# Attention and gated recurrence in one stage: products of pairs as reductions, backward states read from PSUM at the readout, and a written table of steps

## The chip, the cores and the metric

The kernel runs on one core of one Trainium2 chip. The metric is device time in microseconds (us) of one execution; the number compared is the median over several executions. Engines: PE is TensorE (matrix products and transposes), DVE is VectorE, ACT is ScalarE, POOL is GpSimd, and SP issues DMAs.

## The reference

One layer of a diffusion backbone on 2048 latent and 256 context tokens: a modulated norm, one input projection, two groups of heads, an output projection, then a SwiGLU network. The first group is softmax attention of 2048 queries over 2304 keys, 8 query heads on 2 key heads of width 64. The second is a gated linear recurrence with 4 heads of 128 by 128 states, run forward and backward:

```python
def gla_chunked(q, k, v, logf, s0):
    """S_t = diag(f_t) S_{t-1} + k_t v_t^T, o_t = S_t^T q_t, chunkwise."""
...
S, o = lax.scan(step, s0, (to_chunks(q), to_chunks(k), to_chunks(v), to_chunks(logf)))
...
ox_f, _ = gla_chunked(*hgrn2_prep(qx, ix, ffx, lb_l[0]), sc_f)
ox_b, _ = gla_chunked(*map(flip, hgrn2_prep(qx, ix, fbx, lb_l[1])), sc_b)
o = rmsnorm(o_f + flip(o_b), gain).reshape(Bn, T, HG_WIDTH)
return (o * jax.nn.silu(g.astype(jnp.float32))).astype(g.dtype)
```

Each latent scan starts from the last context state of its own direction. All is float32.

## The kernel before

The program has stages for the projections, then one stage that does the attention and the recurrence together, then the output projection and the SwiGLU network. The change lies in the middle stage.

**Attention.** The work is 64 items, two heads for 128 queries each; round r of the loop handles item r, so there are 64 rounds (r = 0 to 63), and a last pass that finishes. Names carry the item: `neg11_0_1_0` is item (query block 11, key head 0, second pair), its first head. A round has six places j = 0 to 5, one for each third of the 2304 keys of each of the two heads. At a place PE multiplies the scores s (128 x 768, two PSUM buffers), DVE takes their minimum `neg`, ACT takes the exponential into `pr` and sums it. After three thirds, ACT makes two factors `fac` for a head, POOL multiplies two thirds of `pr` by them, and the sums `ls` are multiplied by them later, in `finish`. PE transposes the `pr` of the item before into `pt` (two PSUM buffers, shared with `pof`), ACT or DVE copies them to `pf`, and at the round's end PE makes the products `av`, which ACT copies to `ot`; in the next round `finish` transposes `ot` into `pof`, and DVE divides (`oo`).

**Recurrence.** A `Unit` is one head and 512 latent tokens (u = 1 to 4) or the 256 context tokens (u = 0). `F03` is the forget gate of head 0, unit 3, with both directions as its last axis. A unit starts in the rounds 1, 4, 8, 11, 15 and so on to 53, and goes through seven levels, one a round. A level multiplies neighbouring pairs of decays into a tile T of half the size (DVE, line 685; at level 0 it reads F), and POOL and ACT make the next M, C and Q from T. F has one buffer, loaded by SP. The score blocks `pa` of two units at a time go into PSUM, and DVE copies them into A under a mask. After seven levels the unit is closed: `keys` transposes M and C (`pk`, copied to `kt` by ACT), `forward` multiplies with the values V (`psf`) and carries the state S along on DVE, `backward` makes the products `psb`, which ACT copies to `dS`. When a head's four units are closed, `head_out` carries the backward states `Sb` from the last chunk to the first on DVE, PE makes the outputs `po`, and each is normalised: ACT squares it, DVE sums, `rstd_from` makes the factor (on DVE the line `ms`, on POOL the power `rs`), DVE multiplies by QSCALE and then the output by `rs`, POOL multiplies by the gate `gt`, and SP stores it.

**What sets the order.** PE runs in the order of the code. For DVE, ACT, POOL and SP a scheduler sets the order from its own costs when the program is built; each engine then works through its queue in that order and waits where an operand is late. The pool `ps_h` has two PSUM buffers for all of pk, psf, psb, po, pa, pd and av. Closing and readout steps stand in a list, and `slots` spreads them over the places of a round by their number.

Of the kernel before, what the change touches and what calls it, by code (L numbers as in the profile page):

```python
# [16 lines left out]
P = 128  # L17
# [51 lines left out]
def block_kernel(ctx: ExitStack, tc: tile.TileContext, a: dict, out: bass.AP, dbg=None):  # L69
# [46 lines left out]
    def rstd_from(sp, ss, n, width, name):  # L116

        ms = sp.tile([P, width], F32, tag="ms", name=f"ms_{name}")
        nc.vector.tensor_scalar(ms, ss, 1.0 / n, EPS, op0=ALU.mult, op1=ALU.add)  # L119
        rs = sp.tile([P, width], F32, tag="rs", name=f"rs_{name}")  # L120
        nc.gpsimd.tensor_tensor(rs, ms, mhalf[:, :width], op=ALU.pow)  # L121
        return rs
# [446 lines left out]
    with ExitStack() as st:  # L569
# [17 lines left out]
        for lv in range(7):  # L587
            mf = up.tile([P, P], F32, tag="kt", name=f"mf{lv}", bufs=4)
            nc.sync.dma_start(mf, a["k_mask"][:, lv, :])
            nc.vector.tensor_copy(mask[:, lv, :], mf)  # L590
        class Unit:
# [59 lines left out]
            def level(self, pa=None):  # L651
# [32 lines left out]
                T3 = Tt[:, :nb, :].rearrange("p (j s) d -> p j s d", s=2)  # L684
                nc.vector.tensor_tensor(T2, T3[:, :, 0, :], T3[:, :, 1, :], op=ALU.mult)
# [3 lines left out]
            def keys(self, d):  # L689
# [6 lines left out]
                kt = up.tile([P, 512], F32, tag="kt", name=f"kt{h}{u}{d}", bufs=4)  # L696
# [17 lines left out]
            def backward(self, V):  # L714
# [8 lines left out]
        def head_out(h, V, S, units):  # L723
            Tt, dSb = units[0].T, units[0].dS
            coef, add = [Tt[:, 0, 1:2], dSb[:, 1, :]], dSb[:, 0, :]

            def chain(u):

                nonlocal coef, add
                out = []  # L730
                for c in range(3, -1, -1):
                    g = (u - 1) * 4 + c
                    Sb = smh.tile([P, P], F32, tag="Sb", name=f"Sb{h}_{g}", bufs=8)
                    nc.vector.scalar_tensor_tensor(Sb, coef[1], coef[0], add, op0=ALU.mult, op1=ALU.add)
                    coef, add = [units[u].T[:, c, 1:2], Sb], units[u].dS[:, c, :]
                    out.append(Sb)
                return out

            states = chain(4)
            for u in range(4, 0, -1):  # L740
                A, Q = units[u].A, units[u].Q
                po = ps_h.tile([P, 512], F32, tag="h", name=f"po{h}{u}")
                for c in range(3, -1, -1):
                    g = (u - 1) * 4 + c
                    cs = slice(c * P, (c + 1) * P)
                    nc.tensor.matmul(po[:, cs], A[:, cs], V[:, g + 2, :], start=True, stop=False)
                    nc.tensor.matmul(po[:, cs], Q[:, 1, cs], S[:, g + 2, :], start=False, stop=False)
                    nc.tensor.matmul(po[:, cs], Q[:, 0, cs], states[3 - c], start=False, stop=True)
                if u > 1:
                    states = chain(u - 1)  # L750
                o = up.tile([P, 512], F32, tag="o", name=f"o{h}{u}", bufs=2)
                o3 = o.rearrange("p (c v) -> p c v", v=P)
                p3 = po.rearrange("p (c v) -> p c v", v=P)
                nc.scalar.activation(o, po, AF.Square)
                ss = smh.tile([P, 4], F32, tag="ss4", name=f"sso{h}{u}")
                nc.vector.tensor_reduce(ss, o3, axis=AX.X, op=ALU.add)
                rs = rstd_from(smh, ss, P / QSCALE ** 2, 4, f"o{h}{u}")
                nc.vector.tensor_scalar(rs, rs, QSCALE, None, op0=ALU.mult)
                gt = up.tile([P, 4, P], F32, tag="gt", name=f"gt{h}{u}", bufs=1)
                nc.sync.dma_start(gt, s_g[h // 2][(u - 1) * 512:u * 512, (h % 2) * P:(h % 2 + 1) * P]  # L760
                                  .rearrange("(c p) v -> p c v", p=P))
                yield "open"
                nc.vector.tensor_tensor(o3, p3, rs[:, :, None].to_broadcast([P, 4, P]), op=ALU.mult)
                nc.gpsimd.tensor_tensor(o3, o3, gt, op=ALU.mult)
                nc.sync.dma_start(s_hg[h][(u - 1) * 512:u * 512].rearrange("(c p) v -> p c v", p=P), o3)
                yield

        class Recurrence:
# [3 lines left out]
            def __init__(self):  # L772
                self.lanes = {}
                self.steps, self.open = [], None
                self.V, self.S, self.units = {}, {}, {}
                self.starts = {1 + 7 * (n // 2) + 3 * (n % 2): n for n in range(4 * NH)}
                self.made = {}
                self.ctx = {}
# [16 lines left out]
            def closing(self, n, ctx):  # L795


                u, h = self.made.pop(n), n // 4
                V, S = self.V[h], None
                u.keys(0)  # L800
                yield
                u.keys(1)
                yield
                if n % 4 == 0:
                    S = self.S[h] = hp.tile([P, NTOK // P + 1, P], F32, tag="S", name=f"S{h}")
                    ctx.forward(V, S)
                    yield
                u.forward(V, self.S[h])
                yield
                u.backward(V)  # L810
                self.units[h][u.u] = u
                yield

            def closing_context(self, c):
                c.keys(0)
                yield
                c.keys(1)
                yield
                c.backward(self.V[c.h])
                self.units[c.h] = {0: c}  # L820
                yield

            def begin(self, r):
# [13 lines left out]
                n = self.starts.get(r - 7)  # L837
                if n is not None:
                    self.steps.append((self.closing(n, self.ctx.get(n // 4)), 4 + (n % 4 == 0)))
                n = self.starts.get(r - 3)  # L840
                if n is not None and n % 4 == 0:
                    self.steps.append((self.closing_context(self.ctx[n // 4]), 3))
                n = self.starts.get(r - 7)
                if n is not None and n % 4 == 3:
                    self.steps.append((head_out(n // 4, self.V[n // 4], self.S[n // 4], self.units[n // 4]), 4))

            def prepare(self, r):
                if r in self.starts:
                    self.made[self.starts[r]].prepare()

            def diagonal(self, r):
                if r in self.starts:
                    self.made[self.starts[r]].diagonal()
                    return True

            beside = iter(())

            def slots(self, r):


                due = sum(n for _, n in self.steps)
                left = next((i for i in range(1, 8) if r + i in self.starts), 2)
                k = -(-due // left)
                if r in self.starts:
                    return (0, 1, 4, 2)[:max(k, 2)]
                return ((), (2,), (1, 3), (0, 2, 4), (0, 1, 3, 4), (0, 1, 2, 3, 4))[min(k, 5)]

# [714 lines left out]
```

## Time and profile before

| | |
|---|---|
| Median of 3 runs | 3433.66 us (3432.63 to 3435.47) |
| The profiled execution | 3434.58 us, span 3432.8 us |
| PE busy in the span | 3246.4 us (95%) |
| DVE, ACT, POOL busy | 1940.3, 1605.0, 1781.2 us |
| Attention stage | 724 to 1885 us, PE busy 1049.6 |
| Mean granted PE clock | 0.982 |

The profile is one execution; lines such as L685 are those of the program before. A row of a group gives its busy time, the mean length of one in ns, and the time its engine stood idle just before such instructions, with what ended the waits. In a list of waits, the numbers are the total in us, how often, and the longest. PEclk is the clock that PE was granted, as a share of full speed; busy times of one engine include its time at a lower clock.

### The profile page before, as it was taken

What the parts mean: (1) busy time and instruction counts of PE and PEld (TensorE: products, weight loads), DVE (VectorE), ACT (ScalarE), POOL (GpSimd) and SP (SyncE); (2) the same over time, 40 slices, a digit from 0 to 9 for tenths busy, and PEclk for the clock granted to TensorE, in tenths of its full rate; (3) what the DMA queues carried; (4) which work ended last, traced back from release to release, by engine and by line L of the source; (5) the groups of instructions that cost most, each with busy time, mean ns of one, the idle gap of its engine ahead of it and who ended that gap; (6) DMA issues with size and microseconds to landing.
All of it is one profiled execution on the core that took longest, in us unless ns stands there. A gap on an engine that the chain in (4) does not pass through costs nothing. (4 is left out here: it accounts for less than half of the span.)

```text
span 3432.8 us, 54945 instructions
## 1 busy us (share of the span) xinstructions
PE 3246.4 (95%) x20220; PEld 2692.7 (78%) x20220; DVE 1940.3 (57%) x3302; ACT 1605.0 (47%) x3343; POOL 1781.2 (52%) x1616
## 2 busy tenths in 40 slices
PE   8999999989898888998999998999989989999998
PEld 5998987977777777777777887788867768888887
DVE  6444555136667667767666556444466753333566
ACT  4322322247676676776775214333344543333444
POOL 4322232137777777877755107767732257666322
PEclk9999999999999999999999999999989999999999
DMA  7244655421112102111104443544475543333764
GB/s 237 92 142 138 174 165 160 139 87 33 35 30 63 42 29 75 51 34 46 33 24 133 144 136 107 172 153 144 159 255 184 178 145 104 104 96 98 250 199 163
DMA packets 358623, 408.05 MB, mean 119 GB/s; under 512 B 31856, under 2 KB 249936, under 8 KB 358096
## 3 DMA queue, kind: packets, MB, share of 16 engines
q1 hardware_dynamic: 358352, 404.53, 37.0%
q8 instruction: 159, 2.61, 0.3%
q14 instruction: 112, 0.92, 0.1%
HBM read 274.92 MB, written 129.52 MB: 118 GB/s over the span
## 5 line engine op out<-in xcount | busy, mean ns | idle before, releaser
L933 DVE TENSOR_REDUCE neg<-s 128x1 f32<-128x768 f32 x384 | 365.8, 954 | 208.6 <-PE s L930 207.2
L945 POOL TENSOR_TENSOR pr<-pr,fac 128x768 f32<-128x768 f32 x256 | 372.8, 1478 | 127.8 <-ACT fac L941 124.0
L930 PE MATMUL s<-K,qs 128*128 128x512 f32 (+1 forms) x1536 | 374.7, 367 | 43.9 <-ACT pr L938 42.7
L938 ACT ACTIVATE pr<-s,neg 128x768 f32<-128x768 f32 x384 | 349.7, 911 | 95.3 <-DVE neg L933 69.0
L953 PE MATMUL pt<-identr,pr 128*128 128x128 f32 x2304 | 337.3, 279 | 46.2 <-DVE oo L989 21.6
L930 PEld LDWEIGHTS s<-K,qs 128*128 128x128 f32 x1536 | 265.4, 193 | 119.8 <-ACT pr L938 59.4
L953 PEld LDWEIGHTS pt<-identr,pr 128*128 128x128 f32 x2304 | 265.7, 143 | 65.5 <-ACT pf L959 26.4
L959 ACT ACTIVATE pf<-pt 128x512 f32<-128x512 f32 x448 | 259.2, 606 | 77.2 <-PE pt L953 74.9
L967 PE MATMUL av<-pf,V 128*64 128x256 f32 x2304 | 267.6, 387 | 13.0 <-DVE neg L937 6.9
L967 PEld LDWEIGHTS av<-pf,V 128*64 128x64 f32 x2304 | 165.8, 140 | 90.6 <-issue 11.3
L1473 POOL TENSOR_TENSOR y<-y,yg 128x512 f32<-128x512 f32 x48 | 76.1, 1600 | 286.1 <-DVE yg L1472 282.3
L1442 DVE TENSOR_TENSOR x<-lr,x 128x512 fp32r<-128x512 f32 x154 | 119.8, 812 | 67.2 <-ACT x L1441 64.4
L1442 DVE TENSOR_TENSOR dl<-lr,dh 128x512 fp32r<-128x512 f32 x154 | 118.6, 809 | 67.0 <-ACT dh L1441 67.0
L1441 ACT ACTIVATE dh<-lr 128x512 fp32r<-128x512 f32 x154 | 89.4, 623 | 110.8 <-PE pd1A L1496 53.1
L1441 ACT ACTIVATE x<-lr 128x512 fp32r<-128x512 f32 x154 | 90.6, 626 | 93.8 <-PE pd0A L1496 38.5
L343 PE MATMUL f<-hTh,wh 128*128 128x512 f32 (+1 forms) x320 | 121.0, 378 | 6.8 <-ACT ft L372 6.8
L1303 PE MATMUL pA<-x,A11h 128*128 128x512 f32 x352 | 114.8, 407 | 8.2 <-ACT A11h L1276 5.9
L1496 PE MATMUL pd0A<-x,x 128*128 128x512 f32 x528 | 120.7, 389 | 0.0
L343 PE MATMUL f<-hTh,wl 128*128 128x512 f32 (+1 forms) x320 | 119.3, 373 | 0.0
L343 PE MATMUL f<-hTl,wh 128*128 128x512 f32 (+1 forms) x320 | 118.9, 372 | 0.0
L121 POOL TENSOR_TENSOR rs_x<-ms_x,mhalf 128x1 f32<-128x1 f32 x34 | 20.4, 603 | 186.1 <-DVE ms_x L119 186.0
L121 POOL TENSOR_TENSOR rs_qq<-ms_qq,mhalf 128x4 f32<-128x4 f32 x32 | 35.2, 1102 | 156.7 <-DVE ms_qq L119 141.6
(331 smaller groups left out, 9247.6 us busy)
## 6 DMA issues: line engine op xcount, KB each, us to landing
w<-in_w_gu_dram SPq DMA_DIRECT2D x88, 512.0 KB
wm<-in_w_mod_dram SPq DMA_DIRECT2D x24, 1024.0 KB
lr<-s_wT SPq DMA_DIRECT2D x88, 256.0 KB
lr<-in_w_down_dram SPq DMA_DIRECT2D x66, 256.0 KB
s_q<-sq SPq DMA_DIRECT2D x128, 128.0 KB
qs<-s_q SPq DMA_DIRECT2D x32, 512.0 KB
wq<-in_w_down_dram SPq DMA_DIRECT2D x44, 256.0 KB
s_wT<-wq SPq DMA_DIRECT2D x44, 256.0 KB
```

The source lines that it names most:

```text
L343: nc.tensor.matmul(pm[:, :n], w[wi][:, k, c0:c0 + P], hT[b][hi][:, k, :], start=(k == 0 and i == 0), stop=(k == KT - 1 and i == 2))
L930: nc.tensor.matmul(s[:, o:o + w], self.qs[:, hh, self.item[2], half, :], self.kv[0][:, k0 + o:k0 + o + w], start=(half == 0), stop=(half = ...
L933: nc.vector.tensor_reduce(neg[:, i:i + 1], s[:, :n], axis=AX.X, op=ALU.min)
L938: nc.scalar.activation(pr[:, k0:k0 + n], s[:, :n], AF.Exp, bias=neg[:, m:m + 1], scale=-1.0, accum_out=self.ls[:, hh, i:i + 1])
L945: nc.gpsimd.tensor_tensor(pj, pj, self.fac[:, hh, j:j + 1].to_broadcast([P, SW]), op=ALU.mult)
L953: nc.tensor.transpose(pt[:, (2 * i + hh) * P:(2 * i + hh + 1) * P], self.prs[hh][:, (2 * k2 + i) * P:(2 * k2 + i + 1) * P], ident)
L959: nc.scalar.activation(pf, pt, AF.Copy)
L967: nc.tensor.matmul(self.av[i * 64:(i + 1) * 64], self.kv[1][:, 2 * k2 + i, :], self.pf[k2][:, i * 256:(i + 1) * 256], start=(n == 0), stop ...
L1303: nc.tensor.matmul(acc, w[wi][:, k, :], x[xi][k], start=(start and k == 0 and i == 0), stop=(stop and k == KH - 1 and i == 2), skip_group_ ...
L1441: nc.scalar.activation(hi, src, AF.Copy)
L1442: nc.vector.tensor_tensor(lo, src, f32v(hi), op=ALU.subtract)
L1496: nc.tensor.matmul(cur[t], l[:, t * P:(t + 1) * P], r, start=(start and j == 0 and f == 0), stop=(stop and j == NHF - 1 and f == 2), skip_ ...
```

## The change

Six things change in this stage.

1. The product of pairs, T, is made by a `tensor_reduce` with multiplication over the pair instead of a `tensor_tensor` of two halves. The sums of a head and its factors now lie beside each other in one tile `lf`, and `finish` multiplies them in the same way.
2. `backward` no longer runs when a unit is closed. It runs at the readout, its products stay in PSUM, and the state's `scalar_tensor_tensor` reads them there. The copies `dS` go; the context's first state is copied (`Sc`), one 128 x 128 tile a head. The transposed keys `kb` are kept until then, five buffers of 512, and `kt` has three buffers instead of four.
3. `ms` and the QSCALE product of the readout run on POOL instead of DVE.
4. A class `Readout` has the steps `chain` (backward products and four states) and `output` (the twelve products of `po`, the square, the sums, the factor); `store` comes at the next place.
5. A table `plan` gives each closing and readout step its round and place, instead of `slots`. For the first three heads, chains and outputs lie in four rounds from the one after the closing round on; for the last one in two, ending in round 62 instead of 63.
6. The context's keys are made one round later, at places 2 and 4.

```diff
-    def rstd_from(sp, ss, n, width, name):
+    def rstd_from(sp, ss, n, width, name, eng=None):
...
-        nc.vector.tensor_scalar(ms, ss, 1.0 / n, EPS, op0=ALU.mult, op1=ALU.add)
+        (eng or nc.vector).tensor_scalar(ms, ss, 1.0 / n, EPS, op0=ALU.mult, op1=ALU.add)
...
-                T3 = Tt[:, :nb, :].rearrange("p (j s) d -> p j s d", s=2)
-                nc.vector.tensor_tensor(T2, T3[:, :, 0, :], T3[:, :, 1, :], op=ALU.mult)
+                nc.vector.tensor_reduce(T2, Tt[:, :nb, :].rearrange("p (j s) d -> p j d s", s=2),
+                                        axis=AX.X, op=ALU.mult)
...
-                kt = up.tile([P, 512], F32, tag="kt", name=f"kt{h}{u}{d}", bufs=4)
+                kt = kp.tile([P, 512], F32, tag="kb", name=f"kb{h}{u}", bufs=5) if d else \
+                    up.tile([P, 512], F32, tag="kt", name=f"kt{h}{u}", bufs=3)
...
-                self.dS = kp.tile([P, 4, P], F32, tag="dS", name=f"dS{self.h}{self.u}")
-                nc.scalar.activation(self.dS[:, :self.nch, :].rearrange("p c v -> p (c v)"), ps[:, :self.n], AF.Copy)
+                return ps.rearrange("p (c v) -> p c v", v=P)
...
+            def context(self):
+                ps = self.ctx.backward(self.V)
+                c = smh.tile([P, P], F32, tag="Sc", name=f"Sc{self.h}", bufs=2)
+                nc.scalar.activation(c, ps[:, 0, :], AF.Copy)
+                self.state(15, ps[:, 1, :], self.ctx.T[:, 0, 1:2], c)
+
+            def state(self, g, x, coef, add):
+                t = self.states[g] = smh.tile([P, P], F32, tag="Sb", name=f"Sb{self.h}_{g}", bufs=8)
+                nc.vector.scalar_tensor_tensor(t, x, coef, add, op0=ALU.mult, op1=ALU.add)
+
+            def chain(self, u):
+                ps = self.units[u].backward(self.V)
+                for c in range(3, -1, -1):
+                    g = (u - 1) * 4 + c
+                    if g:
+                        self.state(g - 1, self.states[g], self.units[u].T[:, c, 1:2], ps[:, c, :])
...
+                self.rs = rstd_from(smh, ss, P / QSCALE ** 2, 4, f"o{h}{u}", nc.gpsimd)
+                nc.gpsimd.tensor_scalar(self.rs, self.rs, QSCALE, None, op0=ALU.mult)
...
+                        places = [(1, 0), (1, 1), (1, 3), (2, 0), (2, 2), (3, 0), (3, 2), (4, 2)] if h < NH - 1 \
+                            else [(0, 5), (1, 0), (1, 1), (1, 2), (1, 3), (2, 0), (2, 1), (2, 2)]
...
+            def step(self, r, j):
+                if self.late is not None:
+                    self.late[0].store(self.late[1])
+                    self.late = None
+                if (r, j) in self.plan:
+                    f, args = self.plan.pop((r, j))
+                    f(*args)
...
-                                     scale=-1.0, accum_out=self.ls[:, hh, i:i + 1])
+                                     scale=-1.0, accum_out=self.lf[:, hh, i, :1] if i < NSEG - 1
+                                     else self.ls[:, hh, i:i + 1])
...
-            nc.vector.tensor_tensor(ls[:, :, :NSEG - 1], ls[:, :, :NSEG - 1], fac, op=ALU.mult)
+            nc.vector.tensor_reduce(ls[:, :, :NSEG - 1], lf, axis=AX.X, op=ALU.mult)
```

The scheduler's order moves with this. The first place is DVE at the start of round 23, where unit 4 of head 1 has its F loaded (T14 is its T, s0, s1 and s2 the thirds of the scores, psf10 the context's forward products). Before:

```order
L685 TENSOR_TENSOR T14_0_13240<-F14_12819 128x512
L685 TENSOR_TENSOR T14_1_13441<-T14_0_13240 128x256
L933 TENSOR_REDUCE neg11_0_1_0_12617<-s0_11_0_1_0_12618 128x1
L685 TENSOR_TENSOR T14_2_13638<-T14_1_13441 128x128
L685 TENSOR_TENSOR T14_3_13834<-T14_2_13638 128x64
L933 TENSOR_REDUCE neg11_0_1_0_12617<-s1_11_0_1_0_12639 128x1
L709 COPY S1_12653<-psf10_12654 128x128
L989 TENSOR_TENSOR oo10_0_1_12666<-pof10_0_1_12659,li10_0_1_12663 128x256
```

And in the changed program:

```order
L684 TENSOR_REDUCE T14_0_13220<-F14_12806 128x512
L930 TENSOR_REDUCE neg11_0_1_0_12604<-s0_11_0_1_0_12605 128x1
L684 TENSOR_REDUCE T14_1_13421<-T14_0_13220 128x256
L930 TENSOR_REDUCE neg11_0_1_0_12604<-s1_11_0_1_0_12626 128x1
L684 TENSOR_REDUCE T14_2_13611<-T14_1_13421 128x128
L710 COPY S1_12640<-psf10_12641 128x128
L987 TENSOR_TENSOR oo10_0_1_12653<-pof10_0_1_12646,li10_0_1_12650 128x256
```

The second and third product now stand behind the first and the second minimum; the first one stays at its place.

The second place is DVE at the readout of head 0, whose states are Sb0_15 down to Sb0_0, with dS or psb as the products of a unit. Before, in round 20:

```order
L734 SCALAR_TENSOR_TENSOR Sb0_7_12036<-Sb0_8_11963,T03_6_10724,dS03_11291 128x128
L734 SCALAR_TENSOR_TENSOR Sb0_6_12038<-Sb0_7_12036,T02_6_9921,dS02_10417 128x128
L734 SCALAR_TENSOR_TENSOR Sb0_5_12040<-Sb0_6_12038,T02_6_9921,dS02_10417 128x128
L734 SCALAR_TENSOR_TENSOR Sb0_4_12042<-Sb0_5_12040,T02_6_9921,dS02_10417 128x128
L756 TENSOR_REDUCE sso04_11967<-o04_11965 128x4
L933 TENSOR_REDUCE neg10_0_0_1_11984<-s0_10_0_0_1_11985 128x1
L119 TENSOR_SCALAR ms_o04_11969<-sso04_11967 128x4
```

In the changed program, in round 19:

```order
L930 TENSOR_REDUCE neg9_0_1_0_11638<-s0_9_0_1_0_11639 128x1
L740 SCALAR_TENSOR_TENSOR Sb0_14_11658<-Sb0_15_11555,T04_6_11395,psb04_11653 128x128
L684 TENSOR_REDUCE T13_0_12588<-F13_12120 128x512
L740 SCALAR_TENSOR_TENSOR Sb0_13_11660<-Sb0_14_11658,T04_6_11395,psb04_11653 128x128
L930 TENSOR_REDUCE neg9_0_1_0_11638<-s1_9_0_1_0_11673 128x1
L684 TENSOR_REDUCE T13_1_12793<-T13_0_12588 128x256
L740 SCALAR_TENSOR_TENSOR Sb0_12_11662<-Sb0_13_11660,T04_6_11395,psb04_11653 128x128
L684 TENSOR_REDUCE T13_2_12989<-T13_1_12793 128x128
L740 SCALAR_TENSOR_TENSOR Sb0_11_11664<-Sb0_12_11662,T04_6_11395,psb04_11653 128x128
L987 TENSOR_TENSOR oo8_0_1_11718<-pof8_0_1_11711,li8_0_1_11715 128x256
L761 TENSOR_REDUCE sso04_11702<-o04_11700 128x4
L930 TENSOR_REDUCE neg9_0_1_0_11638<-s2_9_0_1_0_11722 128x1
```

The states now begin a round earlier, alternate with the products T13, and read psb04 in PSUM; the sum sso04 of the first output comes ahead of the round's third minimum, and its ms is gone from DVE.

The third place is POOL at the first output of head 0 (Q13 is the product of q and F of a unit that starts soon, pr the multiplication of the exponentials by the factors). Before, in round 20:

```order
L991 TENSOR_TENSOR oo9_0_0_11914<-oo9_0_0_11914 128x128
L945 TENSOR_TENSOR pr10_0_0_0_11865<-pr10_0_0_0_11865,fac10_0_0_11864 128x768 x2
L628 TENSOR_TENSOR Q13_12452<-q13_12138,F13_12136 128x512 x2
L121 TENSOR_TENSOR rs_o04_11971<-ms_o04_11969,mhalf_115 128x4
L764 TENSOR_TENSOR o04_11965<-o04_11965,gt04_11974 128x512
L678 TENSOR_TENSOR Q11_10797<-Q11_10797,T11_4_11848 128x8x32
```

In the changed program, in round 19:

```order
L628 TENSOR_TENSOR Q13_12412<-q13_12122,F13_12120 128x512 x2
L989 TENSOR_TENSOR oo8_0_1_11718<-oo8_0_1_11718 128x128
L119 TENSOR_SCALAR ms_o04_11704<-sso04_11702 128x4
L121 TENSOR_TENSOR rs_o04_11706<-ms_o04_11704,mhalf_115 128x4
L943 TENSOR_TENSOR pr9_0_1_0_11637<-pr9_0_1_0_11637,lf9_0_1_11635 128x768 x2
L763 TENSOR_SCALAR rs_o04_11706<-rs_o04_11706 128x4
L669 TENSOR_TENSOR C11_6_12100<-M11_5_11867,T11_4_11875 128x4x64
L666 TENSOR_TENSOR M12_2_11878<-M12_1_11625,T12_0_11633 128x64x2x2
L772 TENSOR_TENSOR o04_11700<-o04_11700,gt04_11709 128x512
```

The chain ms, rs, QSCALE, o of one output now stands on POOL, and between the power and the QSCALE step lies a pair of pr products of the running item.

On PE the products psb of a head's units leave the rounds 10, 13, 17 and 19 and go to places 3 of round 19, 2 of rounds 20 and 21 (that of unit 4 stays at place 0 of round 19); the outputs po, before at places 2 and 4 of round 20 and 1 and 3 of round 21, are at 1 of round 19, 0 of 20, 0 of 21 and 2 of 22. The other heads repeat this every 14 rounds. At the stage's end, ACT's casts of the output weights (`woh`, from loads `wos`) move from the last pass into round 63.

More of the change, by code (lines that the diff above doesn't have):

```diff
@@ L745, in head_out @@
                     cs = slice(c * P, (c + 1) * P)
[L746 to L751, printed above, removed]
@@ L752, in head_out @@
-                o3 = o.rearrange("p (c v) -> p c v", v=P)
-                p3 = po.rearrange("p (c v) -> p c v", v=P)
+                    nc.tensor.matmul(po[:, cs], A[:, cs], self.V[:, g + 2, :], start=True, stop=False)
+                    nc.tensor.matmul(po[:, cs], Q[:, 1, cs], self.S[:, g + 2, :], start=False, stop=False)
+                    nc.tensor.matmul(po[:, cs], Q[:, 0, cs], self.states.pop(g), start=False, stop=True)
+                o = self.o = up.tile([P, 512], F32, tag="o", name=f"o{h}{u}", bufs=2)
@@ new lines, in __init__ @@
+                self.plan = {}
+                for n in range(4 * NH):
+                    r, h = 8 + 7 * (n // 2) + 3 * (n % 2), n // 4
+                    self.at(r, 0, self.close, n, 0)
+                    self.at(r, 1, self.close, n, 1)
+                    if n % 4 == 0:
+                        self.at(r - 3, 2, self.close_context, h, 0)
+                        self.at(r - 3, 4, self.close_context, h, 1)
+                        self.at(r + 1, 1, self.forward_context, h)
+                        self.at(r + 1, 3, self.forward, n)
+                    elif n % 4 < 3:
+                        self.at(r + 1, 2, self.forward, n)
+                    else:
+                        self.at(r, 2, self.forward, n)
+                        self.at(r, 4, self.readout, h)
+                        steps = [(self.chain, 4), (self.output, 4), (self.chain, 3), (self.output, 3),
+                                 (self.chain, 2), (self.output, 2), (self.chain, 1), (self.output, 1)]
+                        places = [(1, 0), (1, 1), (1, 3), (2, 0), (2, 2), (3, 0), (3, 2), (4, 2)] if h < NH - 1 \
+                            else [(0, 5), (1, 0), (1, 1), (1, 2), (1, 3), (2, 0), (2, 1), (2, 2)]
+                        for (f, u), (d, j) in zip(steps, places):
+                            self.at(r + d, j, f, h, u)
@@ L780, in values, with at @@
+            def at(self, r, j, f, *args):
+                assert (r, j) not in self.plan
+                self.plan[r, j] = f, args
             def values(self, h):
@@ L793, in context, with close, close_context, forward_context @@
                     yield
[L795 to L821, printed above, removed]
+            def close(self, n, d):
+                self.made[n].keys(d)
+            def close_context(self, h, d):
+                self.ctx[h].keys(d)
+            def forward_context(self, h):
+                self.S[h] = hp.tile([P, NTOK // P + 1, P], F32, tag="S", name=f"S{h}")
+                self.ctx[h].forward(self.V[h], self.S[h])
+            def forward(self, n):
+                self.made[n].forward(self.V[n // 4], self.S[n // 4])
+            def readout(self, h):
+                self.heads[h] = Readout(h, self.V[h], self.S[h],
+                                        {u: self.made[4 * h + u - 1] for u in range(1, 5)}, self.ctx[h])
+                self.heads[h].context()
+            def chain(self, h, u):
+                self.heads[h].chain(u)
+            def output(self, h, u):
+                self.heads[h].output(u)
+                self.late = self.heads[h], u
             def begin(self, r):
@@ L836, in begin @@
                     self.beside = self.context(n // 4)
[L837 to L845, printed above, removed]
@@ L847, in prepare @@
-            def prepare(self, r):
-                if r in self.starts:
[L849 to L866, printed above, removed]
@@ L1010, in block_kernel @@
             if item is None:
-                assert not rec.lanes
-                while rec.steps:
-                    rec.step()
-                rec.rest()
+                assert not rec.lanes and not rec.plan and rec.late is None
                 order_T = iter(T_ORDER)
```

90 lines of the change are left out of this document (31 added, 59 removed).

## The prediction

> **What bounds the kernel now.** I read the page first for the span, then the busy time of each engine stretch by stretch through the attention stage, then the waits of that stage, then the groups of DVE instructions, then single stretches in order of time.
>
> ```profile
> span 3432.8 us, 54945 instructions
> ```
>
> The profiled execution took 3434.58 us by its own clock, 0.9 us above the median of the three runs, 3433.66. My sum is made against 3434.6. The attention stage runs from 724 to 1885 us:
>
> ```profile
> core 0: us, PE busy (x) PEld busy (x) DVE busy (x) ACT busy (x) POOL busy (x), PEclk, DMA share, GB/s
> 724.00:1885.00 1161.00, 1049.61 (x9083) 860.13 (x9082) 810.58 (x1364) 808.06 (x1835) 848.22 (x907) 0.97 0.17 51
> 724.00:790.00 66.00, 52.38 (x375) 41.33 (x374) 46.93 (x83) 46.46 (x112) 49.02 (x52) 0.90 0.33 95
> 790.00:1000.00 210.00, 190.54 (x1682) 155.64 (x1681) 141.91 (x227) 148.61 (x337) 155.91 (x168) 0.97 0.12 36
> 1000.00:1200.00 200.00, 177.34 (x1539) 147.38 (x1540) 145.50 (x244) 135.94 (x314) 153.75 (x168) 0.96 0.16 47
> 1200.00:1400.00 200.00, 178.13 (x1602) 145.65 (x1600) 143.34 (x243) 137.96 (x320) 152.45 (x171) 0.98 0.19 56
> 1400.00:1600.00 200.00, 183.54 (x1638) 150.51 (x1638) 143.31 (x249) 147.51 (x340) 154.72 (x172) 0.99 0.12 34
> 1600.00:1800.00 200.00, 186.26 (x1644) 152.80 (x1645) 133.52 (x225) 139.34 (x313) 137.85 (x147) 0.98 0.12 35
> 1800.00:1885.00 85.00, 81.41 (x609) 66.83 (x608) 56.07 (x99) 52.24 (x105) 44.53 (x32) 1.00 0.40 124
> ```
>
> PE is the bound, and two things can be won from it. It stands still for 1161 - 1050 = 111 us. And the granted clock takes more: (1 - clock) times each stretch is 6.6, 6.3, 8, 4, 2, 4 and 0 us, so 24 us after the first stretch. Everything else on PE stays, since no matmul is added or removed. Who keeps PE waiting:
>
> ```profile
> PE s L930 <- ACT pr L938: 42.7, 56, 4.1
> PE pt L953 <- DVE oo L989: 21.6, 14, 4.4
> ...
> PE pt L953 <- DVE pf L957: 8.4, 13, 1.2
> PE av L967 <- DVE neg L937: 6.9, 3, 2.3
> PE av L967 <- DVE o L763: 4.9, 3, 1.6
> PE pa L647 <- DVE o L763: 4.3, 3, 1.4
> ...
> DVE T L685 <- DMA F<-s_f: 29.5, 15, 3.0
> ```
>
> DVE is busy only 811 of 1161 us, yet it ends 46 us of these waits directly, and part of the 42.7, because an exponential waits for its minimum. The reason is in single instructions of DVE:
>
> ```profile
> L933 DVE TENSOR_REDUCE neg<-s 128x1 f32<-128x768 f32 x384 | 365.8, 954 | 208.6 <-PE s L930 207.2
> L685 DVE TENSOR_TENSOR T<-T 128x64 f32<-128x64 f32 (+6 forms) x120 | 71.9, 616 | 18.2 <-POOL Q L680 11.8 <-POOL M L666 4.6 <-POOL C L669 0.3
> L734 DVE SCALAR_TENSOR_TENSOR Sb<-Sb,T,dS 128x128 f32<-128x128 f32 x60 | 37.3, 622 | 4.3 <-PE po L748 2.9
> L984 DVE TENSOR_TENSOR ls<-ls,fac 128x4 f32<-128x4 f32 x64 | 37.1, 580 | 22.8 <-ACT fac L941 22.4
> L685 DVE TENSOR_TENSOR T<-F 128x512 f32<-128x512 f32 (+1 forms) x20 | 31.4, 1570 | 29.5 <-DMA F<-s_f 29.5
> L711 DVE SCALAR_TENSOR_TENSOR S<-S,T,psf 128x128 f32<-128x128 f32 x68 | 23.2, 342 | 8.4 <-PE psf L704 7.6
> L121 POOL TENSOR_TENSOR rs_o<-ms_o,mhalf 128x4 f32<-128x4 f32 x16 | 16.2, 1012 | 8.0 <-DVE ms_o L119 7.6
> L756 DVE TENSOR_REDUCE sso<-o 128x4 f32<-128x512 f32 x16 | 10.9, 682 | 6.5 <-ACT o L754 6.4
> L758 DVE TENSOR_SCALAR rs_o<-rs_o 128x4 f32<-128x4 f32 x16 | 11.4, 711 | 1.8 <-POOL rs_o L121 1.8
> L986 DVE TENSOR_REDUCE li<-ls 128x2 f32<-128x6 f32 x64 | 10.1, 158 | 2.0
> L119 DVE TENSOR_SCALAR ms_o<-sso 128x4 f32<-128x4 f32 x16 | 5.2, 324 | 0.0
> ...
> L685 DVE TENSOR_TENSOR T<-F x20: 424/1115/4356, 733.2 to 1649.0; 128x512 f32<-128x512 f32 x16, 128x256 f32<-128x256 f32 x4
> ```
>
> The 4-number product of L984 takes 580 ns and the 6-number reduction behind it 158. The state product with both tensors in SBUF (L734) takes 622, the same shape with one of them in PSUM (L711) 342. The last row has one product's shortest, median and longest: 0.42, 1.1 and 4.36 us. The longest, in round 26, shows why:
>
> ```profile
> 1188.76 4.36 DVE L685 TENSOR_TENSOR T<-F 128x512 f32<-128x512 f32 x1 [1.12 <-DMA F<-s_f]
> 1193.04 0.94 DVE L933 TENSOR_REDUCE neg<-s 128x1 f32<-128x768 f32 x1
> ...
> 1194.46 1.09 PE L953 MATMUL pt<-identr,pr 128*128 128x128 f32 x4 [4.35 <-DVE oo L989]
> ...
> 1190.02 2.56 POOL L628 TENSOR_TENSOR Q<-q,F 128x512 f32<-128x512 f32 x2
> ```
>
> POOL runs one instruction behind the other until 1192.6, and only then does the DVE product end; the minimum and oo stand behind it, PE waits 4.35 us and restarts slowly. So a DVE instruction with two SBUF tensors waits while POOL works, and reductions do not.
>
> **The change, part by part.**
>
> *Pairs by tensor_reduce.* From 158 ns for 6 inputs and 954 for 768 a reduction costs 152 + 1.04 ns per input; L756, 512 inputs from SBUF, fits (682 measured, 687 by this). It reads both factors as one input, twice the elements: 1221, 687, 420, 286, 219, 186, 169 ns for the seven levels, 3.19 us for a unit, and 2.13 for a context unit of half the size: 16 x 3.19 + 4 x 2.13 = 60 us instead of 71.9 + 31.4 = 103. The ls product becomes one of 8 inputs: 64 x 0.16 = 10 instead of 37. No row shows a reduction that multiplies or that works in pairs; its ends are the fit and twice it (60 more), and I take the fit, which L756 confirms for SBUF input.
>
> *States read from PSUM.* 60 of the 64 go from 622 to L711's 342 ns: 17 us off DVE. The dS copies leave ACT, four copies of 128x128 come; ACT ends no wait that this changes, so 0.
>
> *ms and the QSCALE product go to POOL.* No small product of a tensor with numbers on POOL is in the rows. Its ends are 0.1 us, an instruction with almost nothing in it, and the 1.01 us of the power (L121). I take 0.25, nearer the lower end, because the power itself is the dear part: 32 x 0.25 = 8 us on POOL, which has 313 us to spare. At 1.01 it is 32 us, still covered, unless an output waits for it (below).
>
> In all DVE loses 43 + 27 + 17 us and 5.2 + 11.4 for L119 and L758, 104 of 811. DVE is not the bound, so that isn't the gain. What counts is which PE waits end on it:
>
> A. Waits for oo and pf on DVE, 21.6 + 8.4 = 30.0. In round 26 the first product falls from 4.36 to 1.22, 3.1 of the 4.35 us. The 1.1 us in which DVE stands for the load of F stays, since the product stays at that place in DVE's queue. Other rounds have a smaller blocked part; I take 55%: **-16.5**.
>
> B. Waits of s for an exponential, 42.7. I put down 14, a floor of 0.25 in each of 56, and 9 for the opening rounds without transposes, out of the 13.6 us that PE stands in the first stretch; neither depends on products. Some 19 us are left, which lie in rounds such as 23:
>
> ```profile
> 1135.85 0.93 DVE L685 TENSOR_TENSOR T<-F 128x512 f32<-128x512 f32 x1 [2.42 <-DMA F<-s_f]
> 1136.82 1.57 DVE L685 TENSOR_TENSOR T<-T 128x256 f32<-128x256 f32 x1
> ```
>
> Both stood ahead of the round's first minimum; the new order has one product there, 1.22 us instead of 2.5. The 2.42 us for F stay. Half goes: **-10**.
>
> C. The readout. Two PSUM buffers serve this pool; PE waits 6.9 + 4.9 + 4.3 = 16.1 us in three heads because two outputs follow each other and av and pa need their buffers. The new table spreads them, and each store is tried one place later. But the state chain now holds its PSUM buffer, and in round 19 keys pk101 take the buffer of po04, which DVE frees after three states, a minimum and a fourth state (4 x 0.34 + 0.95 + 0.68 = 3.0 us after psb03), while PE has one s and two groups of transposes before it:
>
> ```profile
> 1187.28 0.96 PE L930 MATMUL s<-K,qs 128*128 128x512 f32 x4
> 1188.07 0.60 PE L953 MATMUL pt<-identr,pr 128*128 128x128 f32 x4
> ```
>
> An s holds PE for 0.79, until the transposes start, and these 0.4 to 0.6 a group: about 1.6, so a new wait of 1.4, and an estimated 0.4 for the state that po04 reads last. -16.1 + 3 x 1.8 = **-10.7**.
>
> D. The clock. Rounds 12, 26 and 40 have the same 139 matmul records:
>
> ```profile
> 925.30:947.70 22.40, 17.47 (x139) 14.28 (x139) 15.28 (x21) 11.67 (x26) 14.45 (x17) 0.85 0.10 27
> 1185.80:1207.70 21.90, 16.97 (x139) 13.89 (x140) 15.34 (x21) 11.67 (x26) 14.45 (x17) 0.92 0.10 28
> 1445.40:1462.50 17.10, 15.36 (x139) 12.28 (x140) 12.19 (x21) 11.57 (x27) 14.86 (x17) 1.00 0.12 37
> ```
>
> The two with a long stand lost clock and are 5 us longer; in the third the product happened to pass quickly, at full clock. Of the 24 us two thirds should go with the waits: **-16**. The Trainium skill ("TensorE: Matmul & The Clock Gate", section "Why this matters for your kernels") ties the drop to idle gaps over about 3 us; by it only the waits in the rows above with a longest of 4 us count, and D would be estimated at 8 instead of 16. The trace has clock 0.85 over a round whose longest wait was 4.35, which fits, and does not separate the two here.
>
> E. The stage's end. The readout of the last head ends one round earlier, and the casts of w_out move into the last full round, ahead of evacuations on ACT's queue; some of them wait for their own loads on SP's queue, behind the last store. PE is at 81.4 of 85 us there, so little can be won: between -2 and +6, I take **+1**.
>
> Sum: -16.5 - 10 - 10.7 - 16 + 1 = -52: 3382 us.
>
> **The rivals.** (1) F is the bound of those rounds: DVE still stands 29.5 us for it, with minima behind. If the products' excess was mostly time in which DVE would have waited anyhow, A and B give 10 and 6, C 6, D 8: 3405. For it: the load ends the wait ahead of the blocked product in round 26; against it: 3.1 us there come after the landing. (2) The change doesn't free DVE: a reduction in pairs waits as the product did, 60 + 62 excess = 122 us, 19 more than now. Then A, B and most of D are gone, C keeps 10.7 less what later minima cost, about 10: 3434, no change. Against it: L756 and L986 are steady. The Trainium skill ("VectorE: DVE Perf Modes", "Rules for kernel authors") speaks for a weaker form: it calls tensor_reduce the slowest DVE operation and says to restructure it away. Unblocked, a product of 256 takes 424 ns here against 687 for the reduction, so the rule is right of the instruction by itself and misses the blocked time. (3) Slower: POOL's chain for an output. In the new order the QSCALE step of a head's first output stands behind a pair of pr products (2 x 1.48 us, waiting for fac), DVE's o waits for it, and pf and the next minimum stand behind o. If all 16 outputs came 2.96 us late, that is +47 against the other -41: 3441; it decides from 2.6 us each. Against it: only the first output of a head has pr between.
>
> **How the numbers follow.** Forecast 0.63, (1) 0.17, (2) 0.08, (3) 0.08, a stall at the stage's end that takes half the gain (3408) 0.04. The low end takes A, B's 19.5, C's 16.1 and all 24 of the clock nearly whole, -82: 3352. The high end lies beyond (1), with E at +6 and reductions in pairs a third dearer: 3418. For this kernel 0.2% is 6.9 us; faster by more 0.86, within it 0.06, slower 0.08.
>
> **What would show it.** Right: T at 1.22 us for 1024 inputs with longest near median, Sb at 0.34, ls at 0.16; PE's waits for oo, pf and o under 20 us together; mean clock in the stage 0.98 or more; PE idle near 75 us. Wrong: T's times spread again; a wait of pk or pa on o over 2 us; DVE waiting for rs_o; ACT waiting for wos in the last round.

## The result and the profile after

The changed kernel takes 3372.87 us (median) against 3433.14 of the kernel before; the ratio is 0.9824, 95% interval 0.9802 to 0.9846, so 60 us less. One of the changed kernel's four executions took 9690.47 us; it counts in the median and not in the ratio. The prediction was 3382 in a range of 3352 to 3418. The profiled execution took 3374.67 us, 59.9 less than that of before. All of the gain lies in the attention stage, which fell from 1161 to 1099 us (before it ends at 1885, after at 1823); what follows it in the span takes 1548 us before and 1550 after. The stage by stretches, with the same columns as before:

```profile
724.00:1823.00 1099.00, 1034.62 (x9057) 849.17 (x9058) 707.73 (x1332) 799.10 (x1817) 847.85 (x939) 0.99 0.19 54
724.00:790.00 66.00, 50.69 (x361) 40.63 (x362) 41.83 (x80) 45.42 (x108) 44.55 (x49) 0.87 0.34 90
790.00:1000.00 210.00, 199.15 (x1798) 161.32 (x1796) 136.69 (x252) 158.84 (x366) 169.16 (x185) 0.99 0.13 39
1000.00:1200.00 200.00, 191.19 (x1711) 158.89 (x1707) 129.67 (x246) 148.25 (x339) 163.03 (x187) 0.99 0.17 49
1200.00:1400.00 200.00, 190.68 (x1748) 157.41 (x1747) 131.31 (x258) 147.79 (x342) 168.75 (x195) 1.00 0.22 63
1400.00:1600.00 200.00, 190.47 (x1728) 158.71 (x1729) 134.72 (x260) 148.36 (x342) 165.33 (x190) 0.99 0.15 42
1600.00:1740.00 140.00, 135.72 (x1186) 109.25 (x1184) 89.54 (x166) 103.52 (x235) 93.78 (x101) 1.00 0.08 24
1740.00:1823.00 83.00, 76.72 (x546) 62.97 (x542) 43.96 (x74) 46.91 (x90) 43.24 (x38) 0.98 0.46 137
```

PE's idle time is 1099 - 1035 = 64 us, 47 less than before. The clock, read to two digits, takes 2.1 + 2 + 0 + 2 + 0 + 1.7 = 8 us after the first stretch, 16 less; in the first stretch it takes 2 more (0.87 against 0.90). Together that is 61, and the stage is 62 shorter. DVE is busy 103 us less (810.6 to 707.7). PE's waits, and DVE's that the prediction named:

```profile
PE s L927 <- ACT pr L935: 37.1, 60, 4.7
PE pt L951 <- ACT pf L957: 12.8, 24, 1.9
PE pk L695 <- DVE Sb L740: 2.7, 3, 0.9
PE po L757 <- DVE Sb L740: 2.3, 3, 0.8
PE pt L951 <- DVE oo L987: 2.1, 3, 1.5
...
PE po L755 <- DVE o L770: 0.6, 2, 0.3
...
DVE T L684 <- DMA F<-s_f: 35.2, 16, 4.1
...
DVE o L770 <- POOL rs_o L763: 6.6, 8, 1.2
```

The 21.6 us for oo are 2.1, and the 16.1 us of the readout for av and pa have become 2.7 + 2.3 + 0.6. The wait for F is still there. Another one has grown that the prediction did not look at: DVE stands 34.9 us for ACT's squares ahead of the sums `sso`, where it stood 6.4 before. What that wait costs was not tried apart. The groups of instructions that the change touches:

```profile
L684 DVE TENSOR_REDUCE T<-T 128x64 f32<-128x128 f32 (+6 forms) x120 | 34.4, 303 | 22.0 <-POOL Q L680 16.6 <-POOL C L669 3.4 <-POOL M L666 1.3
L684 DVE TENSOR_REDUCE T<-F 128x512 f32<-128x1024 f32 (+1 forms) x20 | 22.2, 1112 | 35.2 <-DMA F<-s_f 35.2
L982 DVE TENSOR_REDUCE ls<-lf 128x4 f32<-128x8 f32 x64 | 10.3, 161 | 22.9 <-ACT lf L939 22.6
L740 DVE SCALAR_TENSOR_TENSOR Sb<-Sb,T,psb 128x128 f32<-128x128 f32 x60 | 20.5, 341 | 2.3 <-PE psb L719 1.7
L763 POOL TENSOR_SCALAR rs_o<-rs_o 128x4 f32<-128x4 f32 x16 | 3.7, 230 | 1.4
L119 POOL TENSOR_SCALAR ms_o<-sso 128x4 f32<-128x4 f32 x16 | 3.1, 195 | 18.9 <-DVE sso L761 18.0
```

T takes 34.4 + 22.2 = 57 us instead of 103. The row with the shortest, median and longest of one group (ns) for the products from F:

```profile
L684 DVE TENSOR_REDUCE T<-F x20: 685/1220/1221, 733.4 to 1589.3; 128x512 f32<-128x1024 f32 x16, 128x256 f32<-128x512 f32 x4
```

Median and longest are now the same, 1.22 us, where they were 1.1 and 4.36. The place that the prediction showed in round 26 now reads, in order of time:

```profile
1161.49 2.95 POOL L943 TENSOR_TENSOR pr<-pr,lf 128x768 f32<-128x768 f32 x2
1163.81 1.22 DVE L684 TENSOR_REDUCE T<-F 128x512 f32<-128x1024 f32 x1 [1.13 <-DMA F<-s_f]
1164.34 0.79 POOL L669 TENSOR_TENSOR C<-M,T 128x256 f32<-128x256 f32 x1
1164.95 0.95 DVE L930 TENSOR_REDUCE neg<-s 128x1 f32<-128x768 f32 x1
1165.03 2.61 POOL L628 TENSOR_TENSOR Q<-q,F 128x512 f32<-128x512 f32 x2
1165.81 0.41 DVE L987 TENSOR_TENSOR oo<-pof,li 128x256 f32<-128x256 f32 x1
```

DVE again stands 1.1 us for F, POOL again runs one instruction behind the other, and the reduction ends after 1.22 us beside it.

### The profile page after: what moved, and what is told of

It reads as the page before. It is cut to its first block, busy times and chain, and to the rows that moved or that the text cites. A ratio compares the mean times of both kernels' runs of the same rounds, so it can differ in the third digit from the quotient of the medians.

```text
span 3372.9 us, 54914 instructions
## 1 busy us (share of the span) xinstructions
PE 3233.4 (96%) x20220; PEld 2682.1 (80%) x20220; DVE 1836.1 (54%) x3270; ACT 1597.1 (47%) x3327; POOL 1781.8 (53%) x1648
## 5 line engine op out<-in xcount | busy, mean ns | idle before, releaser
L943 POOL TENSOR_TENSOR pr<-pr,lf 128x768 f32<-128x768 f32 x256 | 370.9, 1472 | 116.2 <-ACT lf L939 116.1
L927 PE MATMUL s<-K,qs 128*128 128x512 f32 (+1 forms) x1536 | 373.2, 366 | 38.5 <-ACT pr L935 37.1
L965 PE MATMUL av<-pf,V 128*64 128x256 f32 x2304 | 260.0, 379 | 0.7 <-DVE neg L934 0.4
L121 POOL TENSOR_TENSOR rs_qq<-ms_qq,mhalf 128x4 f32<-128x4 f32 x32 | 35.2, 1102 | 155.3 <-DVE ms_qq L119 151.2
```

Source lines behind the costliest of these rows:

```text
L927: nc.tensor.matmul(s[:, o:o + w], self.qs[:, hh, self.item[2], half, :], self.kv[0][:, k0 + o:k0 + o + w], start=(half == 0), stop=(half = ...
L943: nc.gpsimd.tensor_tensor(pj, pj, self.lf[:, hh, j, 1:].to_broadcast([P, SW]), op=ALU.mult)
L965: nc.tensor.matmul(self.av[i * 64:(i + 1) * 64], self.kv[1][:, 2 * k2 + i, :], self.pf[k2][:, i * 256:(i + 1) * 256], start=(n == 0), stop ...
```

## The experiments

Every ratio is to the kernel before in the same set of runs; the changed kernel's is 0.9824. Differences in us are a difference of ratios times 3433.

| Kernel | Median us | Ratio, 95% interval |
|---|---|---|
| before, T by reduction | 3401.67 | 0.9920 (0.9902 to 0.9938) |
| before, Q's first products off POOL | 3418.44 | 0.9969 (0.9955 to 0.9982) |
| changed, T by tensor_tensor | 3408.80 | 0.9940 (0.9922 to 0.9958) |
| changed, states from SBUF | 3383.07 | 0.9858 (0.9839 to 0.9876) |
| changed, ls by tensor_tensor | 3388.92 | 0.9870 (0.9849 to 0.9891) |
| changed, ms and QSCALE on DVE | 3378.21 | 0.9847 (0.9827 to 0.9868) |
| the table alone | 3421.41 | 0.9972 (0.9963 to 0.9981) |
| changed, every T twice | 3401.69 | 0.9915 (0.9898 to 0.9932) |
| changed, first T twice | 3382.31 | 0.9863 (0.9850 to 0.9877) |
| changed, two buffers for F | 3356.58 | 0.9786 (0.9766 to 0.9806) |
| two buffers for F, moved places | 3351.93 | 0.9778 (0.9762 to 0.9793) |
| two buffers for F, third pf on DVE | 3345.56 | 0.9755 (0.9742 to 0.9769) |

### Which part made the gain

**The reduction alone**, in the kernel before:

```diff
-                T3 = Tt[:, :nb, :].rearrange("p (j s) d -> p j s d", s=2)
-                nc.vector.tensor_tensor(T2, T3[:, :, 0, :], T3[:, :, 1, :], op=ALU.mult)
+                nc.vector.tensor_reduce(T2, Tt[:, :nb, :].rearrange("p (j s) d -> p j d s", s=2),
+                                        axis=AX.X, op=ALU.mult)
```

> The kernel before with one edit: T by tensor_reduce. My theory (the products of two SBUF tensors were held up by POOL, and minima and oo stood behind them): PE's wait for oo on DVE falls from 21.6 us to under 5, its wait of s for an exponential from 42.7 to about 37, four of the half-speed windows in the rounds with a product go, the readout's waits (16.1 us) stay: about 32 us less than before, 3401. Rival (the table and the states in PSUM made the gain, and the reduction only takes DVE time that was idle anyhow): under 10 us less, 3424 or more.

It takes 27 us off. Its waits, in the list as before:

```profile
PE s L930 <- ACT pr L938: 36.6, 60, 5.4
...
PE av L967 <- DVE neg L937: 7.4, 3, 2.8
PE pt L953 <- DVE oo L989: 6.1, 5, 1.7
PE av L967 <- DVE o L763: 4.9, 3, 1.6
PE pa L647 <- DVE o L763: 4.4, 3, 1.6
```

s falls from 42.7 to 36.6, as expected, oo from 21.6 to 6.1, where under 5 was expected, and the readout's three waits stay (16.7). The clock of the whole execution rises from 0.982 to 0.987.

**The changed kernel without it** (the same lines the other way round):

> The changed kernel with T by tensor_tensor again, all else kept. My theory: the long products come back (longest over 3 us), PE's wait for oo is again near 20 us, and the time rises by about 32 us to 3405. Rival (the table and the PSUM states made the gain): at most 10 us more than the changed kernel, 3383 or less. If both this and the reduction alone move less than 32, the two parts overlap; if more, they need each other.

It costs 40 us of the 60. The row of T from F is again 0.43/1.19/4.33 us, and the waits are 46.1 us for s and 12.0 for oo, where I had expected near 20 for oo. The reduction is worth 27 us alone and 40 beside the other parts. The 12 us between the two are little more than the intervals of the three ratios leave open (about 11), but the trace of the reduction alone shows one reason. There the sums `ls` are still made by tensor_tensor, and one of these products, near the start of the stage, reads:

```profile
775.43 7.16 DVE L984 TENSOR_TENSOR ls<-ls,fac 128x4 f32<-128x4 f32 x1 [1.02 <-ACT fac L941]
```

PE then waits 5.42 us for s and has a clock of 0.51 from 783 to 790 us. In the kernel before, the longest of these products took 1.05 us, and in the changed kernel the sums are reductions. Why the stall shows only beside the reduction of T is open.

**The states from SBUF**, by a copy on ACT, with the table kept:

```diff
-                return ps.rearrange("p (c v) -> p c v", v=P)
+                dS = up.tile([P, 4, P], F32, tag="dS", name=f"dS{self.h}{self.u}", bufs=1)
+                nc.scalar.activation(dS[:, :self.nch, :].rearrange("p c v -> p (c v)"), ps[:, :self.n], AF.Copy)
+                return dS
```

> The changed kernel, its table kept, but the products psb are copied from PSUM to SBUF by ACT at the readout and the states read the copy. My theory: the states go back from 341 to about 600 ns with single ones over 1.2 us (POOL at work), 16 us more on DVE, and PE's wait of po for a state grows from 2.3 us to 6 to 8: 3 to 8 us more than the changed kernel, 3376 to 3381. Rival (the table alone made the readout's gain): within 2 us of it, or less, since psb's buffer comes free a little earlier.

It costs 12 us, more than the 3 to 8 expected, though the two intervals just meet. The state's group, and then the waits that grew:

```profile
L742 DVE SCALAR_TENSOR_TENSOR Sb<-Sb,T,dS 128x128 f32<-128x128 f32 x60 | 38.1, 635 | 2.6 <-ACT dS L722 2.1
```

```profile
PE pt L953 <- DVE pf L957: 6.4, 6, 1.1
PE po L759 <- DVE Sb L742: 5.0, 4, 1.7
PE av L967 <- DVE o L772: 4.8, 3, 1.8
```

Beside po, which was expected, pf and o stand behind the slower states. The copies on ACT are part of this price and were not tried apart.

**The sums by tensor_tensor:**

```diff
-            nc.vector.tensor_reduce(ls[:, :, :NSEG - 1], lf, axis=AX.X, op=ALU.mult)
+            nc.vector.tensor_tensor(ls[:, :, :NSEG - 1], lf[:, :, :, 0], lf[:, :, :, 1], op=ALU.mult)
```

> The changed kernel with the sums multiplied by their factors by tensor_tensor again (64 times four numbers). My theory: the row goes from 161 to near 580 ns, 27 us on DVE, of which a part stands ahead of oo and of minima: 3 to 6 us more, 3376 to 3379. Rival (they lie beside PE's work): within 2 us.

16 us, where I expected 3 to 6. The shortest, median and longest of these 64 products (ns):

```profile
L982 DVE TENSOR_TENSOR ls<-lf x64: 164/375/7153, 752.4 to 1814.3; 128x4 f32<-128x4 f32 x64
```

The longest, in order of time:

```profile
783.61 7.15 DVE L982 TENSOR_TENSOR ls<-lf 128x4 f32<-128x4 f32 x1 [1.02 <-ACT lf L939]
...
790.79 0.16 DVE L984 TENSOR_REDUCE li<-ls 128x2 f32<-128x6 f32 x1
```

And the engines in this stretch (busy time of PE, PEld, DVE, ACT, POOL):

```profile
783.60:790.80 7.20, 4.18 (x30) 3.03 (x26) 7.16 (x2) 3.43 (x8) 7.14 (x9) 0.93 0.00 0
```

Four products per partition took 7.15 us, as long as POOL was busy without a gap (7.14 of 7.20 us). The minima stood behind it, PE waited 5.42 us for s, and its clock was 0.52 from 789.5 to 796.5 us: the same stall as with the reduction alone. From 1000 to 1600 us PE is busy 573 us here and 572 in the changed kernel, so later rounds hardly differ. The stage also began 6 us later (the first of these products at 752.4 instead of 746.7), ahead of any of them, so not all of the 14 us by which this execution is longer belong to the edit. The six runs lie between 3377.64 and 3396.59 us, so how much of the 16 us is the edit's stays open.

**ms and the QSCALE product on DVE:**

```diff
-                self.rs = rstd_from(smh, ss, P / QSCALE ** 2, 4, f"o{h}{u}", nc.gpsimd)
-                nc.gpsimd.tensor_scalar(self.rs, self.rs, QSCALE, None, op0=ALU.mult)
+                self.rs = rstd_from(smh, ss, P / QSCALE ** 2, 4, f"o{h}{u}")
+                nc.vector.tensor_scalar(self.rs, self.rs, QSCALE, None, op0=ALU.mult)
```

> The changed kernel with ms and the QSCALE product back on DVE. My theory: 32 small instructions, 17 us of DVE time that is not on PE's path: 0 to 6 us more, 3375. Rival (POOL's chain holds up the output in the changed kernel): DVE's wait of 6.6 us for rs_o goes and the time falls by up to 6 us.

8 us more, with intervals that overlap: no loss by POOL's chain is seen, and whether moving it gained is not settled.

**The table alone**: the changed kernel with the last four edits together (T by tensor_tensor, states from SBUF, `ls` by tensor_tensor, `ms` and QSCALE on DVE):

> The changed kernel's table of steps alone: T and the sums by tensor_tensor, psb copied to SBUF by ACT and the states read from there, ms and the QSCALE product on DVE. If the parts add up from what their removal cost (36, 16, 10 and 5 us), the time is 3373 + 67 = 3440, so the table alone wins nothing. My theory: the table spreads the readout, so that part of the 16 us of PE's waits for av and pa there still goes, and the prices overlap: about 10 us below the kernel before, 3422. Rival (the table is worth nothing or harms without the cheaper instructions): 3432 to 3440.

10 us less than before, as my theory had it. PE's waits for av and pa in the readout are gone (po waits 6.5 us for states), while s waits 46.9 and oo 14.0.

### What is behind the slow products

**Less work on POOL**, in the kernel before; Q lacks the factor F:

```diff
-                        getattr(nc, QI).tensor_tensor(self.Q[:, 1 - d, :], self.q, F[:, :, d], op=ALU.mult)
+                        nc.scalar.activation(self.Q[:, 1 - d, :], self.q, AF.Copy)
```

> The kernel before, T by tensor_tensor, but the two products of q and F at a unit's start leave POOL: ACT copies q instead, so the factor F in Q is left out. My theory (POOL's work holds the product up): the first product T from F, 0.42/1.1/4.36 us before, has its longest under 2 us, and PE's wait for oo falls from 21.6 to under 12, 10 to 15 us less in all, though ACT gets 32 copies of some 0.6 us. Rival (the product is slow for another reason, such as the landing of F or its stride): the longest stays over 3 us and the time rises with ACT's copies.

T from F, still a tensor_tensor on the same F, loses its long ones, and the time falls by 11 us:

```profile
L685 DVE TENSOR_TENSOR T<-F x20: 447/936/1921, 735.6 to 1634.6; 128x512 f32<-128x512 f32 x16, 128x256 f32<-128x256 f32 x4
```

PE's wait for oo falls from 21.6 to 9.5 us.

So what POOL does beside it sets the length of the product. The rival, F's landing or stride, is the same in both kernels (DVE's wait for F is 27.8 us here and 29.5 before). The later products, beside which POOL still makes M, C and Q, keep their long ones: up to 1.58 us here, 1.57 before.

**T twice**, all products (by a second, equal call), and only the first of a unit, as here:

```diff
+                for _ in range(2 if lv == 0 else 1):
                     nc.vector.tensor_reduce(T2, ...
```

> The changed kernel with each product T made twice by the same tensor_reduce: T takes 113 us of DVE, about the 103 of the kernel before, but evenly. If DVE's total time for T is what counts, the time goes to that of the changed kernel with tensor_tensor, 3409. If single long products and what stands behind them count, which is my theory, each unit's first product is 2.44 us, less than the 4.3 of the long ones but more than the usual 1.2, and the time rises by half of that, 15 to 20 us, to 3390. If neither (DVE has room), under 5.

> The changed kernel with the first product of each unit, T from F, made twice by tensor_reduce; the six others once. It adds 22 of the 57 us of DVE that doubling all of them added. If DVE's amount counts, 22/57 of the 29 us: 11 us more than the changed kernel, 3384. If the place counts (this product stands ahead of a round's first minimum, behind the wait for F), which is my theory: most of it, about 20 us more, 3393. If the later products count (they stand ahead of masks and states, for which av waited 10 us there), under 5.

31 and 13 us. Doubling adds 34.2 + 22.1 = 56 us to DVE, or 22 for the first alone: 0.55 and 0.6 us for each added one. My theory asked for 15 to 20 and then about 20; the simple count of DVE's time gave 36 and 11 and is nearer in both. But it isn't all: T by tensor_tensor takes 68.7 + 26.3 = 95 us in the changed kernel, 38 more than the reduction, and costs 40 us, 1.0 for one. Those products' time, part of it in single pieces of up to 4.3 us, thus cost nearly double; that the length of the pieces is the reason is argued and not shown apart.

### What was left

**Two buffers for F** (and two for kt, for space):

```diff
-                self.F = up.tile([P, 512, 2], F32, tag="F", name=f"F{h}{u}", bufs=1)
+                self.F = up.tile([P, 512, 2], F32, tag="F", name=f"F{h}{u}", bufs=2)
```

> The changed kernel with two buffers for F, and two instead of three for kt. My theory: DVE's 35.2 us of waiting for F, with minima behind it, go nearly to nothing; PE's wait of s for an exponential falls from 37 to about 27, and three of the half-speed windows go: 10 to 14 us less, 3360. Rival (F's wait hides other waits): within 3 us of the changed kernel.

```profile
PE s L927 <- ACT pr L935: 29.6, 54, 5.0
...
DVE T L684 <- DMA F<-s_f: 6.7, 3, 3.4
```

13 us less by the ratios, whose intervals just meet. F's wait falls from 35.2 to 6.7 us, s's from 37.1 to 29.6, and the stage's clock rises from 0.99 to 1.00. DVE's wait for POOL's Q ahead of T grows in return, from 16.6 to 41.5 us. These waits are those of an execution of 3366.51 us, 10 above the median.

**Moved places**, beside it:

```diff
-                        self.at(r - 3, 4, self.close_context, h, 1)
+                        self.at(r - 3, 5, self.close_context, h, 1)
...
-                        places = [(1, 0), (1, 1), (1, 3), (2, 0), (2, 2), (3, 0), (3, 2), (4, 2)] if h < NH - 1 \
-                            else [(0, 5), (1, 0), (1, 1), (1, 2), (1, 3), (2, 0), (2, 1), (2, 2)]
+                        places = [(1, 0), (1, 1), (1, 3), (2, 1), (2, 2), (3, 0), (3, 2), (4, 2)] if h < NH - 1 \
+                            else [(0, 5), (1, 0), (1, 2), (1, 3), (2, 0), (2, 1), (2, 3), (3, 0)]
```

> Two buffers for F as before, and three places moved: the context's second keys from place 4 to 5, the second output of a head from place 0 to 1, and the last head's outputs up to four places later, so that the casts of w_out come later. My theory: PE's waits of pk for a state (2.6 us) and of po go, and the 3.3 us of the last full round shrink: 3 to 6 us less than with two buffers for F alone, 3352. Rival: av and pa meet the moved steps instead, no gain or up to 5 us more.

3 us less, with intervals that overlap, so no gain is shown. The 2.6 us of pk are gone, and a new `PE pa L647 <- ACT kb L698` of 2.5 us stands in their place, where the rival looked for it.

**A third copy of pf on DVE**, with two buffers for F:

```diff
-EV_DVE = (2, 5)
+EV_DVE = (2, 5, 7)
```

> Two buffers for F, and DVE copies three of nine pf tiles instead of two. If DVE's freed time can be put to use, ACT loses 64 x 0.6 us and PE's waits for pf on ACT (11 us) fall: up to 8 us less than with two buffers for F alone, 3349. My theory: DVE's minima come later behind the copy, as the doubled products showed, and the time rises by 5 to 20 us, 3362 to 3377.

My theory was wrong: 11 us less than with two buffers for F alone, though the two intervals just meet, and the fastest of all: 0.9755 of the kernel before, 84 us. Its group of copies, and its first wait:

```profile
L955 DVE COPY pf<-pt 128x512 f32<-128x512 f32 x192 | 131.8, 687 | 34.6 <-PE pt L951 34.4
```

```profile
PE s L927 <- ACT pr L935: 20.2, 26, 4.2
```

DVE gets 44 us of copies, four fifths of what the doubled T added, and PE waits 26 times for s instead of 54. Ahead of its minima DVE stands 156.8 us for PE instead of 204.4, so most of the copies lie where DVE waited for PE. That they cost nothing there is not shown: the same edit takes 64 copies off ACT, whose exponentials s waits for, and PE's wait for oo is back at 4.6 us. The run shows that the relief of ACT outweighs what the copies cost on DVE.

## Why the prediction was right, and where not

| Step | Forecast us | Profile before and after |
|---|---|---|
| A, oo and pf on DVE | -16.5 | oo -19.5; pf on DVE from 8.4 to under 0.3 |
| B, s for an exponential | -10 | 42.7 to 37.1: -5.6 |
| C, readout | -10.7 | 16.1 to 5.6: -10.5 |
| D, clock | -16 | 24 to 8: -16 |
| E, stage's end | +1 | PE idle 3.6 (85 - 81.4) to 6.3 (83 - 76.7): +2.7 |

These changes add up to some 57 of the 59.9 us; the clock of the first stretch, 2 us worse, stands in none of them.

**Durations.** T from F at 1.22, Sb at 341, ls at 161 ns: the fit from reductions to the minimum held for products of pairs. 57 us of T against 60 forecast. On POOL the two small products take 195 and 230 ns, against 250.

**A was too small.** I took 55% of the 30 us; nearly all went. The other 45% were left for waits in rounds with a smaller blocked part, and most of these went too. With the reduction alone 21 of the 30 us are gone: 6.1 us for oo and 2.6 for pf are left.

**B was too large**, because the wait for F stays ahead of the first minimum (35.2 us now); two buffers for F then take 7.5 us off PE's wait for s. Its floor of 14 us, 0.25 in each of 56 waits, which I took as fixed, is not fixed: the third copy on DVE takes 28 of 54 waits and 9.4 of 29.6 us away.

**C came out by its own steps:** the old waits are gone, and the new ones of pk and po are 2.7 + 2.3 us where I had written 3 x 1.8.

**D fits in size**, though its two thirds were a guess. By the Trainium skill ("TensorE: Matmul & The Clock Gate", "Why this matters for your kernels"), which names idle gaps over about 3 us, D was estimated at 8. The trace disagrees: in the changed kernel PE fell to half clock after shorter ones. First PE in order of time, then the stretch that followed (the clock is the last figure but two):

```profile
875.22 0.38 PE L981 MATMUL pof<-identr,ot 128*128 128x128 f32 x2
877.64 1.02 PE L927 MATMUL s<-K,qs 128*128 128x512 f32 x4 [2.04 <-ACT pr L935]
```

```profile
878.40:881.80 3.40, 3.40 (x16) 3.21 (x16) 2.06 (x7) 2.64 (x7) 1.01 (x2) 0.51 0.07 19
```

A stand of 2.04 us ends at 877.6, and from 878.4 the clock is 0.5 for 3.4 us. The two others in the middle of the stage, at 1117 and 1465, follow stands of 1.75 and of 1.68 and 1.02 us.

**"DVE is not the bound, so that isn't the gain"** was the weakest sentence. Added evenly, each us on DVE cost 0.55 to 0.6 us. That is no rate for all of DVE's time, as the third copy shows, but the amount counts too. DVE was busy for 70% of the stage, and that share says nothing of what stands ahead of a minimum.

**The rivals.** F as the bound (1): true in part. DVE still waits for F, and two buffers won 13 us more, but A gave far more than the 10 us of this rival. The reduction waits as the product did (2): no, longest 1.22 us. By the Trainium skill's advice against tensor_reduce ("VectorE: DVE Perf Modes", "Rules for kernel authors") T would have stayed a tensor_tensor; the run without the reduction puts 40 us on that. POOL's chain (3): DVE waits for rs_o 8 times, longest 1.2 us, where 2.6 each would have decided. At the end, ACT waits 2.4 us for wos in the last round and PE 3.3 for pf, as feared, but at that size it is a small term.

## What to carry to other kernels

Look at the shortest and the longest of a group of equal instructions, not its mean: a spread of ten to one can point to an engine that is in the way, and a longer but steady form of the instruction can be the faster one. Cost an engine off the bound by what stands behind its instruction in its queue, not by its busy share: here products added ahead of minima cost more than half their length, and copies that lay mostly in DVE's waits for PE cost less than they won elsewhere. And undo each part of a change in the full version as well as trying it alone: the reduction was worth 27 us in one and 40 in the other, in part because another product's stall showed only once the reduction was in.

## What the hardware showed beyond what was expected

A DVE product of two SBUF operands with four results per partition can take 7.15 us, as long as POOL's instructions follow each other without a gap, while the states with one operand in PSUM took 334 to 349 ns, and ls as a reduction 141 to 167. The Trainium skill ("SBUF — State Buffer", "Who interferes with whom") says that a DVE instruction with two SBUF inputs contends with POOL's reads and that tensor_reduce never does; both agree with the rows here. The 7.15 us lie over eight POOL instructions that follow each other without a gap, so the wait goes over many of them and not just the one that runs. It is not there each time: 64 equal products had a median of 0.375 us.
